# Queries of the dilated attention patterns copied residue by residue on GpSimd, for a stationary block without gaps

## The chip, the cores and the metric

One core of a Trainium2 chip runs the whole program in one launch. The metric is the device time of one execution in microseconds (us). Engines are named as in the profile: PE is TensorE's matmul part, PEld its weight load (the load of the stationary block), DVE VectorE, ACT ScalarE, POOL GpSimd, SP SyncE, which issues nearly all DMAs.

## What is computed

One layer of a hybrid decoder for a prompt of 2048 tokens (width 1024) and a group of 32 sample tokens. The part that matters here is the attention of the prompt: 8 heads of 64 dims, three patterns of (window, dilation), outputs merged by their softmax denominators.

```python
DIL_PATTERNS = ((128, 1), (512, 4), (2048, 16))

def _dilated_branch_prompt(q, k, v, dilation, slopes):
    qs = q.reshape(b, L, dilation, h, dh)      # token = j * dilation + c
    ks = k.reshape(b, L, dilation, h, dh)
    ...
    scores = jnp.einsum('bnqchd,bnkchd->bnchqk', qb, kb).astype(jnp.float32) * (HEAD_DIM ** -0.5)
    bias = -slopes[:, None, None] * (dilation * diff).astype(jnp.float32)[None]
    scores = jnp.where(valid[None, :, None, None], scores + bias[None, None, None], NEG)
    m = jnp.max(scores, axis=-1, keepdims=True)
    p = jnp.exp(scores - m)
    l = jnp.sum(p, axis=-1, keepdims=True)
    out = jnp.einsum('bnchqk,bnkchd->bnqchd', (p / l).astype(v.dtype), vb)
```

With dilation r the tokens fall into r residue classes c; within a class, 128 queries attend to their own block of 128 keys and the block before it. Around the attention stand an input projection with a pooling mixer (before it), and the output projection, a norm and a convolutional feed-forward (behind it).

## The kernel before

The stages follow one another: projections (to about 443 us), prompt attention head by head (443 to 841 us), merge of the patterns and output projection (to 1065 us), feed-forward (to the end). Products are made of a high and a low part of the numbers.

In the attention, a head's queries and keys lie in SBUF as the tile `QK`, [128, 3, 2048]: plane 0 holds the queries (64 rows high part, 64 rows low part), planes 1 and 2 the keys' high and low part. Columns are tokens in their natural order. There are two such tiles, so the next head's is loaded (by SP) during the current head.

The work of the attention is cut into 192 items (head h, pattern p, pair pr): 8 heads, 3 patterns (dilation 1, 4, 16; called p0, p1, p2 below), 8 pairs of query blocks. `advance(i)` issues three things:

- `scores` of item i: per block (idx = 2 * pr + s) two products into `Sp` in PSUM, L262 with the keys' high part and L263 with the low part. The stationary operand of both is the block of 128 queries, the moving operand the 128 or 256 keys. `views` cuts both out of `QK` with a stride of r columns: 1 in p0, 4 in p1 (16 bytes), 16 in p2 (64 bytes). Then DVE adds the bias table and finds the extreme (L265, tile `T`), ACT takes the exponential (L267, tile `Pt`).
- `turn` of item i - 2: PE transposes the blocks of `Pt` (L275), DVE or ACT copies them to SBUF (L278, L280, tile `PTs`).
- `values` of item i - 3: products with the values `V` (L296; fp32, so each is two instructions), copied out by ACT (L300), the extremes `st` by POOL (L302). Every fourth item a half of the pattern's output goes to HBM.

Per head p0 has 31 blocks of 128 keys by 128 queries, p1 28 and p2 16. So 128 blocks of p2 in all (8 heads x 16) and 32 of p1 (the 4 first of each head) have 128 keys, the other 96 of p1 have 256.

The order in which each engine's instructions stand is set at build time by the framework's scheduler; each engine then works its list off in order. POOL's list in this stage is short: 128x8 copies of `st`, memsets of a column in `V`, one bias table per head (L166). SP's list has the loads of `QK` and `V`, the stores of the outputs, small parameter rows (tile `row`), eight pieces of W_out for later (tile `rawo`), and a load of the pooling mixer's result (`act<-pl_s`).

Of the kernel before, what the change touches and what calls it, by code (L numbers as in the profile page):

```python
# [9 lines left out]
F32 = mybir.dt.float32  # L10
# [33 lines left out]
def kernel(ctx, tc, ins, cst, outs):  # L44
# [24 lines left out]
    nc.vector.memset(mhalf, -0.5)  # L69
    # the sample group's columns of a product stand side by side, hi then lo: one pass takes both  # L70
    mix_s = const.tile([P, 4, 2 * NSMP], F32R, name="mix_s")
# [22 lines left out]
    def norm_rows(pool, xt, g_bc, bufs, tag="xn"):  # L94
        """x * rsqrt(mean(x^2) + eps), times g_bc where given."""
        rows = xt.shape[0]
        xn = pool.tile([rows, DM], F32, tag=tag, name="xn", bufs=bufs)
        ss = pool.tile([rows, 1], F32, tag="ss", name="ss", bufs=2)
        nc.scalar.activation(xn, xt, AF.Square, accum_out=ss)
        r = rms_scale(pool, ss, 1, DM)  # L100
        if g_bc is None:
            nc.scalar.activation(xn, xt, AF.Copy, scale=r)
        else:
            nc.vector.scalar_tensor_tensor(out=xn, in0=xt, scalar=r, in1=g_bc[:rows], op0=ALU.mult, op1=ALU.mult)  # L104
        return xn
# [5 lines left out]
    def transpose_split(src, hi, lo):  # L111
        """src [n, DM] -> hi, lo [128, KT, n]."""
        n = src.shape[0]
        for h in range(2):
            tp = psum.tile([P, 4, P], F32, tag="tp", name="tp", bufs=4)
            for k in range(4):
                kk = 4 * h + k
                nc.tensor.transpose(tp[:, k, :n], src[:, kk * P:(kk + 1) * P], ident[:n, :n])  # L118
            split(hi[:, 4 * h:4 * h + 4, :], lo[:, 4 * h:4 * h + 4, :], tp[:, :, :n])
# [8 lines left out]
    class Later:  # L128
        """Work on the tensor engine that is issued some bursts of products after what it waits for."""

# [38 lines left out]
    def value_tile(pool, tag):  # L169
        """Pairs of heads, with a column of ones on either side (the sums of the weights)."""  # L170
        t = pool.tile([P, 16, P + 2], F32, tag=tag, name="V", bufs=3 if tag == "V" else 1)
        nc.gpsimd.memset(t[:, :, 0:1], 1.0)
        nc.gpsimd.memset(t[:, :, P + 1:P + 2], 1.0)
        return t
# [15 lines left out]
    def param_load(j):  # L190
        n = 2 * NF if j < 4 else 2 * SB
        row = rows_of[j] = p2.tile([2 * NF, 4 * P], F32, tag="row", name="row", bufs=3)
        if j < 4:
            src = conv_b if j == 3 else conv_w[0, j:j + 1]
            nc.sync.dma_start(row[:, 0:P], src.rearrange("l (c p) -> (l c) p", p=P))
        else:
            nc.sync.dma_start(row[:n], stv[:, (j - 4) * 4 * P:(j - 3) * 4 * P])
# [16 lines left out]
    def store_o(p, hp, O, half):  # L214
# [9 lines left out]
        else:  # L224
            eng.dma_start(dst.rearrange("(i c) f -> i c f", c=16)[:, s], O[:, s])

    def load_head(h):
        qk, tab = qk_tile(), bias_table(h)
        load_qk(h, qk, slice(0, S))
        heads[h] = (*(qk[:, i, :] for i in range(3)), tab)  # L230

    pair_v, pair_o, heads = {}, {}, {}

    def next_v(hp, p):
        pair_v[hp, p] = value_tile(p2, "V")
        load_v(hp, p, pair_v[hp, p])

    def views(h, p, idx):
        r = DILS[p]
        blk, c = divmod(idx, r)  # L240
        q, kh, kl = (x.rearrange("p (j c) -> p c j", c=r)[:, c, :] for x in heads[h][:3])
        lo = blk - 1 if blk else 0
        return (q[:, blk * P:(blk + 1) * P], kh[:, lo * P:(blk + 1) * P], kl[:, lo * P:(blk + 1) * P],
                ([idx - r] if blk else []) + [idx])
# [3 lines left out]
    def scores(it):  # L248
        h, p, pr = it
        tab = heads[h][3]  # L250
        if pr % 4 == 0:
            state["st"] = pq.tile([P, 8], F32, tag="st", name="st", bufs=4)
        st = state["st"]
        Sp = psum.tile([P, 2, 2 * P], F32, tag="mm", name="Sp", bufs=4)
        Pt = pq.tile([P, 2, 2 * P], F32, tag="P", name="Pt", bufs=4)
        blocks = []
        for s in range(2):
            idx = 2 * pr + s
            i8 = idx % 8
            q, kh, kl, kb = views(h, p, idx)  # L260
            w = P * len(kb)
            nc.tensor.matmul(Sp[:, s, :w], q, kh, start=True, stop=False)  # L262
            nc.tensor.matmul(Sp[:, s, :w], q, kl, start=False, stop=True)  # L263
            T = pq.tile([P, 2 * P], F32, tag="T", name="T", bufs=4)
            nc.vector.tensor_tensor_reduce(out=T[:, :w], in0=Sp[:, s, :w], in1=tab[:, p, 2 * P - w:], op0=ALU.add,  # L265
                                           op1=ALU.min, scale=1.0, scalar=3e38, accum_out=st[:, i8:i8 + 1])
            nc.scalar.activation(Pt[:, s, :w], T[:, :w], AF.Exp, bias=st[:, i8:i8 + 1], scale=-1.0)  # L267
            blocks += [(s, idx % 4, n, b, len(kb)) for n, b in enumerate(kb)]
        return st, Pt, blocks
# [38 lines left out]
    attn, PTs = {}, {}  # L308

    def advance(i):  # L310
        if i < len(items):
            attn[i] = scores(items[i])
        if 0 <= i - 2 < len(items):
            PTs[i - 2] = turn(items[i - 2], attn[i - 2])
        if 0 <= i - 3 < len(items):
            values(items[i - 3], attn.pop(i - 3), PTs.pop(i - 3))

# [1 line left out]
    right = ExitStack()  # L319
    pw = right.enter_context(tc.tile_pool(name="pw", bufs=1, side="right"))  # L320
    with tc.tile_pool(name="p1", bufs=1) as p1:
# [24 lines left out]
        def load_w(i):  # L346
            """Raw weights; the high part of the next ones takes their place."""
            j = JS[i]
            for c in range(KT // 2):
                raw[j, c] = (pw.tile([P, 2, AW], F32, tag=f"w{i}{c}", name="raw", bufs=1) if i < 3 else  # L350
                             p1.tile([P, 2, AW], F32, tag="x" if c == 2 else "ue", name="raw", bufs=2))
                nc.sync.dma_start(raw[j, c], wv[:, 2 * c:2 * c + 2, j * AW:(j + 1) * AW])

        def split_w(i):
            """hi + lo of gain * w."""
            j = JS[i]
# [120 lines left out]
        def window_sums(cur, g, pick, tag, shape, n):  # L477
            """Trailing sums over 2 << g columns by doubling; pick(tile, a, b) are the columns a..b-1."""
            sh = 1
# [148 lines left out]
    cw = const2.tile([P, 4, 2 * NF], F32, name="cw")  # L628
    # rows 0..15: the sample group's states (new ones take the place of the old), 16, 17: the prompt's
    stT = const2.tile([P, 2 * NF, 2 * SB + 2], F32, name="stT")  # L630
# [3 lines left out]
    def h_tile(k):  # L634
        """High and low part of 128 rows: of W_out at first, then of the normed tokens of a chunk."""
        return ph.tile([P, 2, TM], F32R, tag=f"h{k}", name="h", bufs=1)
# [12 lines left out]

# [1 line left out]
    with tc.tile_pool(name="p2", bufs=1, reuse_waits="tile") as p2:  # L651
        wo0 = [h_tile(k) for k in range(KT)]
        next_v(0, 1)
        next_v(0, 2)
        nc.vector.memset(stT[:, :, 2 * SB:], 0.0)
        for i in range(AHEAD, len(items) + 3):
            if i < len(items):
# [12 lines left out]
                if h == 6 and (8 * p + pr) % 3 == 0:  # L670
                    for k in ((8 * p + pr) // 3,):
                        raw = p2.tile([P, CH], F32, tag="row", name="rawo", bufs=3)
                        nc.sync.dma_start(raw, wov[:, k, 0:CH])
# [7 lines left out]
    with tc.tile_pool(name="p4", bufs=1, reuse_waits="tile") as p4:  # L681
# [19 lines left out]

# [1 line left out]
        wo = [[[wo0[k][:, b, 0:CH] for b in range(2)] for k in range(KT)], {}]  # L703
# [119 lines left out]

# [1 line left out]
        ST = p4.tile([P, 3, H, SB, SN], F32, name="ST")  # L825
# [19 lines left out]
        def cache_rows(c, b, n, p, near):  # L845
            """The 128 cached rows that query n of sequence b reads in pattern p, as [128, AW]."""
            if p == 0:
# [138 lines left out]
        def sample_mix():  # L986
            """Output projection, residual and norm of the sample group, then its columns hs_s."""
            y = smp["y"] = p4.tile([NSMP, DM], F32, tag="ya", name="ya", bufs=5)
# [48 lines left out]
        def store_ffn_state(j):  # L1037
            """New states of 512 columns, the sample group's and the prompt's."""
            tp = psum.tile([P, 4, P], F32, tag="tp", name="tpf", bufs=4)
# [17 lines left out]
        for c in range(NCHUNK):  # L1057
# [5 lines left out]
            def spread(pss, prompt, sample):  # L1063
                """Pairs (destination, PSUM source) of the prompt's and sample's columns."""
                if not last:
# [159 lines left out]
```

## Time and profile before

| what | value |
|---|---|
| median of 3 runs | 2590.65 us (2588.75 to 2595.58) |
| profiled execution, first to last instruction (span) | 2587.3 us |
| PE / PEld / DVE / ACT / POOL busy share of the span | 99% / 85% / 67% / 42% / 5% |
| prompt attention, from the first to the last score product | 443 to 841 us |
| DMA, mean over the span | 152 GB/s |

The profile gives of its own execution the span alone; the median of the runs stands 3.35 us above it. Busy time of PE counts overlapping matmuls by modelled ends, so a busy PE is not PE at its peak; how far apart instructions start says more. [...]

### The profile page before, as it was taken

The page shows a single profiled execution, that of the slowest core. Times are in us where ns is not written, and L with a number is a line of the kernel's source. Part 1 is how long each engine was busy: PE and PEld are TensorE (multiplying, and loading weights), DVE is VectorE, ACT ScalarE, POOL GpSimd, SP SyncE. Part 2 cuts the span into 40 slices and gives each one's busy share as a digit, 9 for nine tenths or more (in the row PEclk, how much of TensorE's full clock was granted, in tenths as well). Part 3 has the DMA queues.
Part 4 walks back from the last instruction along what each step waited for, and adds up shares of the span by engine and source line. Part 5 has one row for each costly group of instructions (what it writes and reads, how often), then busy time and mean ns, then how long its engine had stood idle before and what let it go on. Part 6 is the DMA issues. An engine that isn't in the chain of part 4 may idle for free.

```text
span 2587.3 us, 35898 instructions
## 1 busy us (share of the span) xinstructions
PE 2556.2 (99%) x13310; PEld 2187.1 (85%) x13310; DVE 1727.8 (67%) x3819; ACT 1089.6 (42%) x2021; POOL 117.4 (5%) x160
## 2 busy tenths in 40 slices
PE   8999999999999999999999999999999999999999
PEld 5888887999999788788888888888888788999997
DVE  7444345555555676799887788887887666666665
ACT  6333232555555222434433464443444443444442
POOL 1111111000000200000000000000000000000000
PEclk9999999998998999999999999999999999999999
DMA  6333335765561897955557534447443337232321
GB/s 220 106 118 112 121 110 149 153 174 131 125 160 51 294 309 244 298 183 183 181 165 233 157 106 146 137 128 246 143 138 114 122 110 232 84 90 83 91 75 61
DMA packets 411738, 393.57 MB, mean 152 GB/s; under 512 B 15211, under 2 KB 318407, under 8 KB 408876
## 3 DMA queue, kind: packets, MB, share of 16 engines
q1 hardware_dynamic: 411340, 390.48, 49.8%
q8 instruction: 105, 1.72, 0.3%
q0 software_dynamic: 224, 0.80, 0.1%
q14 instruction: 69, 0.57, 0.1%
HBM read 305.70 MB, written 85.52 MB: 151 GB/s over the span
## 4 chain that ended last, share of the span: by engine, by line
PE 62%; DMA 1%; DVE 1%; issue 0%; ACT 0%; SPq 0%; POOL 0%; POOLq 0%
PE pu L973 38%; PE pd L1149 19%; PE po L752 3%; PE pd L1143 1%; DMA om<-o_s 0%; DMA h<-hn_s 0%; PE sacc L925 0%; PE sacc L924 0%; PE po L1006 0%; DMA raw<-in_w_up_dram 0%; PE tp L118 0%; DMA h_s<-ya 0%; PE tpf L1041 0%; DVE xn L104 0%; PE tpa L737 0%
## 5 line engine op out<-in xcount | busy, mean ns | idle before, releaser
L973 PE MATMUL pu<-h,w 128*128 128x512 f32 (+1 forms) x5232 | 989.0, 349 | 1.5 <-ACT w L108 1.0
L973 PEld LDWEIGHTS pu<-h,w 128*128 128x128 f32 x5232 | 849.9, 188 | 132.4 <-ACT w L108 1.4
L1149 PE MATMUL pd<-w,act 128*128 128x512 f32 x2112 | 490.2, 392 | 0.0
L1149 PEld LDWEIGHTS pd<-w,act 128*128 128x128 f32 x2112 | 396.6, 188 | 88.1
L108 ACT CAST w<-raw 128x1024 fp32r<-128x1024 f32 (+1 forms) x282 | 286.9, 1026 | 293.0 <-PE pd L1149 189.7
L109 DVE TENSOR_TENSOR w<-raw,w 128x1024 fp32r<-128x1024 f32 (+1 forms) x278 | 328.6, 1185 | 23.9 <-ACT w L108 23.7
L422 PE MATMUL ps<-W_hi,xh 128*128 128x512 f32 x1024 | 332.1, 397 | 1.3 <-ACT xh L108 1.3
L1117 DVE SCALAR_TENSOR_TENSOR cv<-ex,cw,cv 128x512 f32<-128x512 f32 x352 | 262.3, 745 | 29.7 <-ACT cv L1109 27.2
L1107 ACT COPY ex<-pu 128x512 f32<-128x512 f32 (+1 forms) x220 | 110.1, 501 | 350.7 <-PE pu L973 350.3
L265 DVE CUSTOM_DVE_ANT_0 T<-Sp,tab 128x256 f32<-128x256 f32 (+1 forms) x384 | 132.0, 365 | 186.1 <-PE Sp L263 142.2
L422 PEld LDWEIGHTS ps<-W_hi,xh 128*128 128x128 f32 x1024 | 192.2, 189 | 43.4 <-ACT xh L108 2.0
L267 ACT ACTIVATE Pt<-T,st 128x256 f32<-128x256 f32 (+1 forms) x384 | 164.9, 458 | 136.4 <-DVE st L265 134.9
L422 PE MATMUL ps<-W_lo,xh 128*128 128x512 f32 x512 | 202.6, 396 | 0.0
L1151 DVE TENSOR_TENSOR ya<-ya,pd 128x512 f32<-128x512 f32 x192 | 131.0, 683 | 103.7 <-PE pd L1149 102.9
L296 PE MATMUL Op<-V,PTs 128*128 128x65 f32 x1200 | 174.8, 281 | 0.7 <-DVE PTs L278 0.6
L262 PE MATMUL Sp<-QK 128*128 128x256 f32 (+1 forms) x384 | 170.0, 453 | 5.5 <-DMA QK<-kT_hi 3.1
L296 PEld LDWEIGHTS Op<-V,PTs 128*128 128x128 f32 x1200 | 170.0, 209 | 1.2 <-DVE PTs L278 0.7
L1109 ACT ACTIVATE cv<-pu,cw 128x512 f32<-128x512 f32 (+3 forms) x264 | 166.0, 649 | 0.0
L91 POOL TENSOR_TENSOR rs<-ms,mhalf 128x1 f32<-128x1 f32 (+3 forms) x68 | 76.4, 1124 | 1582.7 <-DVE stT L1110 1046.9
L263 PE MATMUL Sp<-QK 128*128 128x256 f32 (+1 forms) x384 | 145.4, 387 | 0.6 <-DMA QK<-kT_lo 0.6
L275 PE MATMUL tp<-ident,Pt 128*128 128x128 f32 x600 | 127.7, 299 | 0.0
L108 ACT CAST act<-cv 128x512 fp32r<-128x512 f32 x88 | 54.6, 621 | 159.4 <-DVE cv L1126 150.7
(220 smaller groups left out, 2637.6 us busy)
## 6 DMA issues: line engine op xcount, KB each, us to landing
raw<-in_w_up_dram SPq DMA_DIRECT2D x176, 512.0 KB
raw<-in_w_down_dram SPq DMA_DIRECT2D x80, 512.0 KB
hn_s<-w SPq DMA_DIRECT2D x16, 1024.0 KB
h<-hn_s SPq DMA_DIRECT2D x32, 512.0 KB
far<-in_cache_k_dram SPq DMA_DIRECT2D x64, 256.0 KB
far<-in_cache_v_dram SPq DMA_DIRECT2D x64, 256.0 KB
om<-o_s SPq DMA_DIRECT2D x16, 792.0 KB
raw<-in_w_in_dram SPq DMA_DIRECT2D x16, 512.0 KB
```

The costliest lines, as they stand in the source:

```text
L108: nc.scalar.copy(hi, src)
L109: (eng or nc.vector).tensor_tensor(out=lo, in0=src, in1=f32(hi), op=ALU.subtract)
L262: nc.tensor.matmul(Sp[:, s, :w], q, kh, start=True, stop=False)
L263: nc.tensor.matmul(Sp[:, s, :w], q, kl, start=False, stop=True)
L265: nc.vector.tensor_tensor_reduce(out=T[:, :w], in0=Sp[:, s, :w], in1=tab[:, p, 2 * P - w:], op0=ALU.add, op1=ALU.min, scale=1.0, scalar=3e ...
L267: nc.scalar.activation(Pt[:, s, :w], T[:, :w], AF.Exp, bias=st[:, i8:i8 + 1], scale=-1.0)
L296: nc.tensor.matmul(Op[:, i4, :], PT[:, j, :], pair_v[hp, p][:, b, v0:v0 + DH + 1], start=n == 0, stop=n == m - 1)
L422: nc.tensor.matmul(ps, xh[:, a, k, :], (W_hi, W_lo)[b][j, k // 2][:, k % 2, :], start=n == 0, stop=n == 3 * KT - 1)
L973: nc.tensor.matmul(ps[:, :n], w[:, a, k, :], hs[k][:, b, c0:c0 + n], start=i == 0, stop=i == 3 * KT - 1)
L1109: nc.scalar.activation(d, s, AF.Identity, bias=cw[:, 3, ct:ct + 1], scale=cw[:, 2, ct:ct + 1])
L1117: nc.vector.scalar_tensor_tensor(out=d, in0=e[j], scalar=cw[:, j, ct:ct + 1], in1=d, op0=ALU.mult, op1=ALU.add)
L1149: nc.tensor.matmul(ps, act[0][:, a, k, tau * P:(tau + 1) * P], wd[k][:, b, :], start=k == 0 and j == 0, stop=k == n - 1 and j == 2)
```

## The change

GpSimd copies the queries of p1 and p2 into a new tile `qs`, half a pattern (1024 columns, 8 blocks) at a time, so that a block's 128 queries lie side by side. There are two such tiles and 32 copies (8 heads x 2 patterns x 2 halves). A copy is issued three items ahead of the first that reads it. The score products of p1 and p2 take their stationary block from `qs`; the moving keys still come from `QK` with the stride. To make room, `Pt` and `T` have 3 buffers in place of 4, `row` (also used by `rawo`) 2 in place of 3.

```diff
-        row = rows_of[j] = p2.tile([2 * NF, 4 * P], F32, tag="row", name="row", bufs=3)
+        row = rows_of[j] = p2.tile([2 * NF, 4 * P], F32, tag="row", name="row", bufs=2)
...
+    def spread_q(h, p, half):
+        qs = spread[h, p, half] = p2.tile([P, S // 2], F32R, tag="qs", name="qs", bufs=2)
+        q, r = heads[h][0], DILS[p]
+        if p == 1:
+            src = q[:, half * (S // 2):(half + 1) * (S // 2)].rearrange("p (b j c) -> p b c j", b=2, c=r)
+            dst = qs.rearrange("p (b c j) -> p b c j", b=2, c=r)
+        else:
+            src = q.rearrange("p (j c) -> p c j", c=r)[:, half * r // 2:(half + 1) * r // 2]
+            dst = qs.rearrange("p (c j) -> p c j", j=P)
+        nc.gpsimd.tensor_copy(dst, src)
...
+    def queries(h, p, idx):
+        if p == 0:
+            return heads[h][0][:, idx * P:(idx + 1) * P]
+        return spread[h, p, idx // 8][:, idx % 8 * P:(idx % 8 + 1) * P]
+
     def views(h, p, idx):
         r = DILS[p]
         blk, c = divmod(idx, r)
-        q, kh, kl = (x.rearrange("p (j c) -> p c j", c=r)[:, c, :] for x in heads[h][:3])
+        kh, kl = (x.rearrange("p (j c) -> p c j", c=r)[:, c, :] for x in heads[h][1:3])
         lo = blk - 1 if blk else 0
-        return (q[:, blk * P:(blk + 1) * P], kh[:, lo * P:(blk + 1) * P], kl[:, lo * P:(blk + 1) * P],
+        return (queries(h, p, idx), kh[:, lo * P:(blk + 1) * P], kl[:, lo * P:(blk + 1) * P],
                 ([idx - r] if blk else []) + [idx])
...
-        Pt = pq.tile([P, 2, 2 * P], F32, tag="P", name="Pt", bufs=4)
+        Pt = pq.tile([P, 2, 2 * P], F32, tag="P", name="Pt", bufs=3)
...
-            T = pq.tile([P, 2 * P], F32, tag="T", name="T", bufs=4)
+            T = pq.tile([P, 2 * P], F32, tag="T", name="T", bufs=3)
...
+    SPREAD = 3
+
     def advance(i):
+        if i + SPREAD < len(items):
+            h, p, pr = items[i + SPREAD]
+            if p and pr % 4 == 0 and i + SPREAD >= 2 * AHEAD:
+                spread_q(h, p, pr // 4)
         if i < len(items):
             attn[i] = scores(items[i])
...
+        for half in range(2):
+            spread_q(0, 1, half)
         for i in range(AHEAD, len(items) + 3):
```

On POOL, in the first head: the difference of the two lists, behind the first small copy of `st`. The memsets prepare value tiles `V`, `O_first<-st` and `O<-st` are small copies.

```order
 L172 MEMSET V 128x16
 L173 MEMSET V 128x16
+L237 COPY qs<-QK 128x1024
 L172 MEMSET V 128x16
 L173 MEMSET V 128x16
-L302 COPY O_first<-st 128x8
-L302 COPY O<-st 128x8 x4
+L237 COPY qs<-QK 128x1024
+L319 COPY O_first<-st 128x8
+L237 COPY qs<-QK 128x1024
+L319 COPY O<-st 128x8
```

Two query copies now stand ahead of the second small copy of `st`; from there on a query copy and a small copy alternate for a while, four query copies per head.

On PE, in p2 of the second head, the list of before (`Sp` score products, `tp` transposes, `Op` products with the values):

```order
L262 MATMUL Sp<-QK 128x128
L263 MATMUL Sp<-QK 128x128
L275 MATMUL tp_5034<-ident,Pt 128x128 x2
L296 MATMUL Op<-V,PTs 128x65 x2
L262 MATMUL Sp<-QK 128x128
L263 MATMUL Sp<-QK 128x128
L262 MATMUL Sp<-QK 128x128
L263 MATMUL Sp<-QK 128x128
```

and of the change:

```order
L279 MATMUL Sp<-QK,qs 128x128
L280 MATMUL Sp<-QK,qs 128x128
L292 MATMUL tp_5050<-ident,Pt 128x128 x2
L313 MATMUL Op<-V,PTs 128x65 x2
L279 MATMUL Sp<-QK,qs 128x128
L280 MATMUL Sp<-QK,qs 128x128
L279 MATMUL Sp<-QK,qs 128x128
L280 MATMUL Sp<-QK,qs 128x128
```

The rows stand in the same order; what differs is that the products also read `qs`, so that PE now waits for POOL's copy.

## Rows read from the trace of the kernel before

**Rows 1.** First part of the page: engine, busy us, share of the span, instructions.
```profile
PE 2556.2 (99%) x13310; PEld 2187.1 (85%) x13310; DVE 1727.8 (67%) x3819; ACT 1089.6 (42%) x2021; POOL 117.4 (5%) x160
```
**Rows 2.** Busy time by stretch: length, each engine's busy us (instructions), clock, DMA, GB/s.
```profile
443.00:841.00 398.00, 394.26 (x2585) 381.70 (x2586) 211.73 (x932) 213.28 (x533) 23.94 (x75) 0.89 0.57 137
```
**Rows 3.** PEld in order of time, p0 of the second head: start, us, line, operation.
```profile
500.29 0.19 PEld L262 LDWEIGHTS Sp<-QK 128*128 128x128 f32 x1 [0.34 <-DVE st L265]
500.40 0.19 PEld L263 LDWEIGHTS Sp<-QK 128*128 128x128 f32 x1
500.52 0.53 PEld L296 LDWEIGHTS Op<-V,PTs 128*128 128x128 f32 x4
```
**Rows 4.** PEld in order of time, p2 of the second head.
```profile
535.20 0.29 PEld L262 LDWEIGHTS Sp<-QK 128*128 128x128 f32 x1
535.39 0.31 PEld L263 LDWEIGHTS Sp<-QK 128*128 128x128 f32 x1
535.61 0.32 PEld L262 LDWEIGHTS Sp<-QK 128*128 128x128 f32 x1
535.84 0.31 PEld L263 LDWEIGHTS Sp<-QK 128*128 128x128 f32 x1
536.09 0.21 PEld L275 LDWEIGHTS tp<-ident,Pt 128*128 128x128 f32 x2
536.27 0.52 PEld L296 LDWEIGHTS Op<-V,PTs 128*128 128x128 f32 x4
536.85 0.30 PEld L262 LDWEIGHTS Sp<-QK 128*128 128x128 f32 x1
```
**Rows 5.** PE in order of time, p1 of the second head.
```profile
516.98 0.58 PE L262 MATMUL Sp<-QK 128*128 128x256 f32 x1
517.38 0.42 PE L263 MATMUL Sp<-QK 128*128 128x256 f32 x1
517.61 0.42 PE L262 MATMUL Sp<-QK 128*128 128x256 f32 x1
517.86 0.41 PE L263 MATMUL Sp<-QK 128*128 128x256 f32 x1
518.09 0.62 PE L275 MATMUL tp<-ident,Pt 128*128 128x128 f32 x4
```
**Rows 6.** PE in order of time, p2 of the second head.
```profile
535.20 0.46 PE L262 MATMUL Sp<-QK 128*128 128x128 f32 x1
535.49 0.39 PE L263 MATMUL Sp<-QK 128*128 128x128 f32 x1
```
**Rows 7.** Who waited for whom, 440 to 845 us: total us, times, longest.
```profile
PEld Sp L262 <- DVE st L265: 7.1, 20, 0.7
```
**Rows 8.** Groups of POOL by shape: busy us, mean ns of one.
```profile
L166 POOL TENSOR_SCALAR tab<-base 128x768 f32<-128x768 f32 x8 | 17.3, 2170 | 1.2 <-DMA base<-const_dram 1.0
L302 POOL COPY O<-st 128x8 f32<-128x8 f32 x44 | 9.0, 205 | 303.3 <-DVE st L265 294.8 <-DMA V<-v_s 8.5
```
**Rows 9.** POOL in order of time, first head.
```profile
453.32 0.19 POOL L302 COPY O_first<-st 128x8 f32<-128x8 f32 x1 [16.15 <-DVE st L265]
```
**Rows 10.** Groups of DVE while POOL made a bias table, 594.2 to 596.2 us, and before, 588 to 594.1 us.
```profile
L265 DVE CUSTOM_DVE_ANT_0 T<-Sp,tab 128x128 f32<-128x128 f32 x1 | 0.3, 292 | 0.2 <-PE Sp L263 0.2
L265 DVE CUSTOM_DVE_ANT_0 T<-Sp,tab 128x128 f32<-128x128 f32 x7 | 2.0, 292 | 3.5 <-PE Sp L263 2.7 <-PE tp L275 0.5
```
**Rows 11.** DVE and POOL in order of time, merge stage.
```profile
854.55 0.69 DVE L731 TENSOR_TENSOR at<-at,t 128x512 f32<-128x512 f32 x1
860.68 2.71 DVE L731 TENSOR_TENSOR at<-at,t 128x512 f32<-128x512 f32 x1
860.38 2.46 POOL L109 TENSOR_TENSOR w<-raw,w 128x1024 fp32r<-128x1024 f32 x1 [1.02 <-ACT w L108]
```
**Rows 12.** Busy time by stretch, second head: p2, its end, and the start of p0.
```profile
526.00:538.00 12.00, 11.94 (x80) 11.41 (x78) 6.65 (x32) 6.01 (x16) 0.57 (x4) 1.00 0.35 95
539.00:545.00 6.00, 6.00 (x31) 6.00 (x30) 2.74 (x15) 3.25 (x9) 0.71 (x2) 0.50 0.63 178
545.00:549.00 4.00, 4.00 (x21) 4.00 (x20) 1.46 (x7) 1.35 (x4) 1.62 (x1) 0.50 1.01 211
549.00:556.00 7.00, 7.00 (x62) 6.78 (x61) 4.81 (x20) 4.59 (x11) 0.37 (x3) 1.00 0.82 195
```

More of the change, by code (lines that the diff above doesn't have):

```diff
@@ L230, in load_head @@
         heads[h] = (*(qk[:, i, :] for i in range(3)), tab)
-    pair_v, pair_o, heads = {}, {}, {}
+    pair_v, pair_o, heads, spread = {}, {}, {}, {}
     def next_v(hp, p):
@@ L671 @@
                     for k in ((8 * p + pr) // 3,):
-                        raw = p2.tile([P, CH], F32, tag="row", name="rawo", bufs=3)
+                        raw = p2.tile([P, CH], F32, tag="row", name="rawo", bufs=2)
                         nc.sync.dma_start(raw, wov[:, k, 0:CH])
```

## The prediction

> **What bounds the kernel now.** I read the page first, then busy time by stretch, then single instructions of PE and its weight loads in order of time, then POOL. The page shows PE busy 99% of the span and POOL 5% [rows 1]. The change touches the prompt attention alone, 443 to 841 us: in these 398 us PE is busy 394.3 and PEld 381.7 us, DVE and ACT 212 and 213 us, POOL 23.9 us [rows 2]. So TensorE sets this stage, and its longest wait for another engine before a score product sums to only 7.1 us [rows 7]. The stages behind it are run by PE as well, and nothing in them is tied to a date: a microsecond saved here should move them forward whole.
>
> Within TensorE, look at how far apart weight loads start, since they run one after another while matmuls overlap them. In p0, where queries lie side by side, loads start 0.11 and 0.12 us apart and last 0.19 us [rows 3]. In p2, where they lie 64 bytes apart, the four loads of an item start 0.19 to 0.25 us apart (0.89 us for four steps, 0.22 each) and last 0.29 to 0.32 us [rows 4]. Same instruction, same 128 columns; only the stride differs. That is what the change removes. [...]
>
> **The change part by part.**
>
> Score products with 128 keys. There are 160 strided blocks of this kind (128 in p2, 32 in p1) with two loads each, 320 loads. A step falls from 0.22 us to what is then the longer of the load (0.11 to 0.12) and the matmul over 128 strided key columns. The latter is not shown alone. From below it is bounded by the contiguous step, 0.11. From above by half of what 256 strided columns take at most, 0.23 to 0.25 us a step in p1 [rows 5], so 0.12. I take 0.12: 320 x 0.10 = **32 us**. If instead such a matmul took the whole 0.22, as a rival assumes, this would shrink.
>
> Score products with 256 keys, 96 blocks in p1. Steps inside a chain of four are 0.23 to 0.25 us, and the last one, whose next load is a contiguous one for a transpose, is still 0.23 [rows 5]; so the moving keys, still strided, seem to hold it, and contiguous queries win nothing there. But the first product of a chain stands 0.40 us ahead of the second in p1 and 0.29 us in p2, where there are half the keys [rows 5, 6]: one load that nothing hides (0.2), plus the matmul. That load loses 0.10. In PE's list 75 of the 96 blocks start such a chain: 75 x 0.10 = **7.5 us**. Between nothing for the rest and a drop to the contiguous step (0.11 less, on 192 products less those 75) lie 0 and 13 us; I take 0, nearest to the 0.23 of that last step.
>
> Query copies, 32 on POOL. No row shows a strided copy. The nearest is the bias table, 128x768 in 2.17 us, 2.8 ns a column, so 2.9 us for 1024 [rows 8]. From above: TensorE pays twice for a stride [rows 3, 4], which would make 5.8 us; far above, the 128x8 copies take 205 ns, 26 ns a column [rows 8], nearly all fixed cost. I take 3 us, 96 us in all beside 398 us in which POOL works 24: hidden. When must a copy be ready? There are two tiles, so the copy for a half starts when the half before the last has been read, four items ahead of its first reader. An item of p2 takes 1.65 us now (first load to first load, 535.20 to 536.85) [rows 4] and about 1.65 - 4 x 0.10 = 1.25 us after. Four of these are 5 us, against 3. In p1 there is more. At the start, POOL's first small copy ends at 453.5 us [rows 9]; two copies behind it end at about 459.5, and p1 begins at about 460 and needs the second half four items later. In POOL's list a small copy that waits for DVE stands between query copies, but these waits are for items that PE has passed by then. So **0 us**.
>
> [...] POOL's copies might slow DVE. In the merge stage a DVE operation with two operands in SBUF took 2.71 us in place of 0.69 while POOL worked [rows 11]. But the score operation L265 has one operand in PSUM, and beside POOL's bias table it took 292 ns, as it did before [rows 10]. The eight splits of W_out pieces in the seventh head have two SBUF operands; POOL will be busy some three eighths of that time, so 3 of them lose 2 us, most of it in DVE's slack: **+2 us**.
>
> Fewer buffers. `Pt` of item i+3 can be overwritten when the transposes of item i are issued, which stand ahead of it in PE's list anyway. `T` with three buffers lets DVE run three blocks ahead of ACT; both are half idle. `row` is needed once in eight items. I count these at 0, and hide the risk in the next term. SP's list changes in that `act<-pl_s` (2 MB) stands some rows earlier, ahead of the third head's `QK` load, whose reader is a head away: 0.
>
> New stalls. DVE's and ACT's 212 us will have to fit in some 358 us, so PE will come early more often; the 7.1 us of waits grow, I say, by **+5 us** (nothing to 15).
>
> The clock. In the second head the granted clock falls from 1.0 to 0.5 near the end of p2, after a stretch with 80 PE instructions in 12 us, and comes back 4 us into p0; at 0.5 the rate is 31 in 6 us and 21 in 4, against 62 in 7 us behind [rows 12]. The stage's mean of 0.89 [rows 2] means 22% of it, 88 us, at the low level. With shorter loads p2 has more matmul work per microsecond and is a quarter shorter, so the falls should come less often. If they went altogether, an item would win some 0.4 us (the level raises transposes and value products, not the strided loads) on the 35 to 40 items in such stretches, 15 us; if they stay, 0. I take about half, **-8 us**.
>
> Sum: -32 - 7.5 + 2 + 5 - 8 = -40.5 us. The span would be 2546.8; with the 3.35 us by which the median stands above it, 2550.2, so **2550 us**.
>
> **Rivals.**
>
> (a) The moving keys bind: a matmul over 128 columns 64 bytes apart takes as long as the load, 0.22. Then only chain starts win: 113 of the 160 narrow blocks and 75 wide ones, 188 x 0.10 = 19 us, less the 5 of stalls and 2 of contention: about 2579 us. For it: the keys stay strided. Against it: a chain starts 0.29 us ahead of its second product with 128 keys, 0.40 with 256 [rows 5, 6], so 128 more columns cost about 0.11.
>
> (b) The moving keys cost nothing, and what I read as their price in p1 was the loads': another 13 us in p1, and full clock, 7 us: about 2530 us. Against it is the step of 0.23 ahead of a contiguous load. [...]
>
> (c) The stride does not matter and the long loads come from something else in p1 and p2: no gain, contention and stalls cover each other, 2591 us. The rows at equal columns [rows 3, 4] speak against it. [...]
>
> (d) POOL is too slow, and slower is the result: PE waits for `qs` at the second half of p2 once a copy takes over 5 us, at its first half over some 7.2 us (four items of p1). Loss per head (C - 5) + (C - 7.2); at C = 8.5 us it eats 38 us, all of the gain. Beyond that the kernel is slower: at 11 us by 78 - 40, some 2629 us. For it: no strided POOL read is in the trace. Against it: C would have to be three times the bias table's price per column.
>
> (e) DVE and ACT catch up with PE in p2, so that half of the narrow term is lost: about 2566 us.
>
> **How the numbers follow.** Forecast 0.60, (a) 0.10, (b) 0.10, (c) 0.05, (d) 0.07, (e) 0.08. The range reaches from (b), with 4 us below it, to just short of (a): 2526 to 2577; it leaves out most of (a), (c), (d). A change of 0.3%, 7.8 us, is about what a measurement of this kernel can tell from none. Faster are the forecast, (a), (b), (e): 0.88, less a little for the edges, 0.87; same (c) 0.05 and that edge, 0.06; slower (d) 0.07.
>
> **What would show it.** Weight loads of the score products at 186 to 192 ns in all patterns; steps of about 0.12 us in p2 and still 0.23 in the middle of p1; query copies of 2.5 to 4 us; no wait of a score product for `qs` worth more than 2 us in all; the attention done in about 358 us with a mean clock of 0.92 or more. I am wrong if p2's steps stay near 0.22, if the copies last over 5 us, or if the time shows up again in the merge stage.

## The result and the profile after

| what | before | after |
|---|---|---|
| median of 4 runs each, side by side | 2589.73 us (2588.75 to 2595.58) | 2545.68 us (2542.25 to 2547.30) |
| ratio, 95% interval | | 0.9825 [0.9811, 0.9839] |
| span of the profiled execution | 2587.3 us | 2545.4 us |
| first to last score product | 443.1 to 841.2 us (398.1) | 441.8 to 796.3 us (354.5) |

The change saves 44 us between the medians and 45 by the ratio, 1.75%; the forecast was 2550 us. In the two profiled executions the span fell by 41.9 us: the attention took 43.6 us less and started 1.3 us earlier, and the stages behind it took 3.0 us more (1746.1 us from the last score product to the end before, 1749.1 after).

The page of after, busy time by engine (compare [rows 1]):

```profile
PE 2509.0 (99%) x13310; PEld 2133.0 (84%) x13310; DVE 1728.4 (68%) x3819; ACT 1086.4 (43%) x2021; POOL 180.5 (7%) x192
```

Busy time by stretch of after, the attention and what lies behind it (compare [rows 2]):

```profile
core 0: us, PE busy (x) PEld busy (x) DVE busy (x) ACT busy (x) POOL busy (x), PEclk, DMA share, GB/s
441.00:797.00 356.00, 346.80 (x2592) 327.57 (x2592) 210.46 (x933) 210.07 (x533) 86.71 (x107) 0.93 0.64 154
797.00:2546.00 1749.00, 1733.81 (x8667) 1459.13 (x8665) 1303.56 (x2406) 711.36 (x1179) 21.48 (x23) 1.00 0.51 161
```

POOL has 63 us more work, PEld 54 us less, and TensorE still sets the stage. DVE and ACT do what they did before.

Weight loads of after in p2 of the second head, in order of time (compare [rows 4]):

```profile
523.98 0.19 PEld L279 LDWEIGHTS Sp<-QK,qs 128*128 128x128 f32 x1
524.09 0.19 PEld L280 LDWEIGHTS Sp<-QK,qs 128*128 128x128 f32 x1
524.20 0.19 PEld L279 LDWEIGHTS Sp<-QK,qs 128*128 128x128 f32 x1
524.31 0.19 PEld L280 LDWEIGHTS Sp<-QK,qs 128*128 128x128 f32 x1
524.45 0.21 PEld L292 LDWEIGHTS tp<-ident,Pt 128*128 128x128 f32 x2
524.63 0.52 PEld L313 LDWEIGHTS Op<-V,PTs 128*128 128x128 f32 x4
525.21 0.19 PEld L279 LDWEIGHTS Sp<-QK,qs 128*128 128x128 f32 x1
```

A load lasts 0.19 us in place of 0.29 to 0.32, the steps are 0.11 us in place of 0.22, and an item takes 1.23 us (523.98 to 525.21) in place of 1.65. The matmuls over 128 strided keys, which the steps of p2 also hold, fit in 0.11 us.

Matmuls of after in p1 of the second head (compare [rows 5]):

```profile
508.17 0.46 PE L279 MATMUL Sp<-QK,qs 128*128 128x256 f32 x1
508.45 0.41 PE L280 MATMUL Sp<-QK,qs 128*128 128x256 f32 x1
508.68 0.41 PE L279 MATMUL Sp<-QK,qs 128*128 128x256 f32 x1
508.91 0.41 PE L280 MATMUL Sp<-QK,qs 128*128 128x256 f32 x1
```

Only the first step of the chain is shorter, 0.28 us in place of 0.40; the others stay at 0.23.

The groups of POOL in the attention of after, by line (busy us, mean ns | idle time before them and what ended it):

```profile
L237 POOL CAST qs<-QK 128x1024 fp32r<-128x1024 f32 x32 | 64.5, 2014 | 143.7 <-PE Sp L280 110.2 <-issue 18.1 <-PE Sp L279 15.4
```

A copy takes 2.01 us. It is the copies that wait for PE, for a free `qs`; a wait of PE for `qs` does not show.

Waits of after in the attention (engine, line, waited for: us in total, times, longest us; compare [rows 7]):

```profile
PEld Sp L279 <- DVE st L282: 8.6, 24, 0.7
...
ACT h L108 <- DMA rawo<-in_w_out_dram: 4.4, 4, 2.7
DVE h L109 <- ACT h L108: 4.1, 4, 2.3
```

The wait for DVE hardly grew. The wait for `rawo` was 0.5 us before: pieces of W_out, which share the smaller `row`, now come late in the seventh head. Where that meets PE, in order of time:

```profile
707.80 0.62 ACT L108 CAST h<-rawo 128x512 fp32r<-128x512 f32 x1 [2.66 <-DMA rawo<-in_w_out_dram]
708.33 0.90 ACT L284 ACTIVATE Pt<-T,st 128x256 f32<-128x256 f32 x2
...
708.88 0.44 PE L292 MATMUL tp<-ident,Pt 128*128 128x128 f32 x2 [2.28 <-ACT Pt L284]
```

ACT, working its list off in order, waits 2.66 us for the piece, the exponentials stand behind it, and PE waits 2.28 us for them.

### The profile page after: what moved, and what is told of

Read it like the earlier page. It is cut to its first block, busy times and chain, and to the rows that moved or that the text cites. A ratio compares the mean times of both kernels' runs of the same rounds, so it can differ in the third digit from the quotient of the medians.

```text
span 2545.4 us, 35989 instructions
## 1 busy us (share of the span) xinstructions
PE 2509.0 (99%) x13310; PEld 2133.0 (84%) x13310; DVE 1728.4 (68%) x3819; ACT 1086.4 (43%) x2021; POOL 180.5 (7%) x192
## 4 chain that ended last, share of the span: by engine, by line
PE 93%; DMA 2%; DVE 2%; issue 1%; ACT 1%; POOL 0%; SPq 0%; DVEq 0%; POOLq 0%; ACTq 0%
PE pu L998 38%; PE pd L1174 19%; PE ps L445 13%; PE po L777 5%; PE Op L313 5%; PE Sp L279 3%; PE tp L292 3%; PE Sp L280 2%; PE tp L118 1%; PE tp L454 1%; PE pd L1168 1%; DVE W_lo L388 1%; DMA QK<-kT_lo 0%; PE pp L519 0%; DMA ya<-in_x_prompt_dram 0%
## 5 line engine op out<-in xcount | busy, mean ns | idle before, releaser
L313 PEld LDWEIGHTS Op<-V,PTs 128*128 128x128 f32 x1200 | 163.6, 202 | 2.7 <-DVE PTs L295 2.0
L445 PEld LDWEIGHTS ps<-W_lo,xh 128*128 128x128 f32 x512 | 96.8, 189 | 20.0
L1135 DVE COPY stT<-ex 128x2 f32<-128x2 f32 x176 | 28.8, 164 | 114.8 <-ACT ex L1132 114.8
```

Of the source, the lines that this page charges most:

```text
L313: nc.tensor.matmul(Op[:, i4, :], PT[:, j, :], pair_v[hp, p][:, b, v0:v0 + DH + 1], start=n == 0, stop=n == m - 1)
L445: nc.tensor.matmul(ps, xh[:, a, k, :], (W_hi, W_lo)[b][j, k // 2][:, k % 2, :], start=n == 0, stop=n == 3 * KT - 1)
```

## The experiments

Each run is compared with the kernel before on the same chip; ratios are to that kernel.

**1. Buffers alone.** The kernel before with the smaller `Pt`, `T` and `row`, and no copies.

```diff
-        ... tag="row", name="row", bufs=3)
+        ... tag="row", name="row", bufs=2)
-        ... tag="P", name="Pt", bufs=4)
+        ... tag="P", name="Pt", bufs=3)
-            ... tag="T", name="T", bufs=4)
+            ... tag="T", name="T", bufs=3)
```

> The kernel before with the smaller buffers alone (Pt and T 3, row 2), no copies, queries still strided. Theory (the gain is the shorter weight loads): 2588 to 2596 us, no gain; score weight loads stay at 290 to 337 ns in p1 and p2. Rival (the gain comes from the other order that the smaller buffers give): some 2550 to 2575 us.

Measured: 2588.75 us, ratio 1.0003 [0.9993, 1.0014]. The buffers cost nothing at the pace of the kernel before.

**2. Copies that nobody reads.** The change, but the products of p1 and p2 take their queries from `QK` as before.

```diff
     def queries(h, p, idx):
-        if p == 0:
-            return heads[h][0][:, idx * P:(idx + 1) * P]
+        if p >= 0:
+            r = DILS[p]
+            blk, c = divmod(idx, r)
+            return heads[h][0].rearrange("p (j c) -> p c j", c=r)[:, c, blk * P:(blk + 1) * P]
```

> The change, but the products of p1 and p2 take their queries from QK with the stride again; the 32 copies are made and read by nobody. Theory (copies are hidden): 2588 to 2598 us, POOL 64 us more. Rival (the copies slow DVE or hold POOL's list, and the change wins in spite of them): over 2600 us. Rival (something else than the reading of the copy wins): below 2580 us.

Measured: 2590.52 us, ratio 1.0007 [0.9996, 1.0019]. POOL is busy 86.6 us in the attention, as in the changed kernel, and it costs at most what the interval leaves, about 5 us. This kernel differs from the changed one only in where the products read their queries, so everything that was won comes from reading the copies.

**3 and 4. One pattern alone.** `queries` as in experiment 2 for the pattern that is left out, and its copies gone.

```diff
-        if p == 0:
+        if p != 2:
...
-            if p and pr % 4 == 0 and i + SPREAD >= 2 * AHEAD:
+            if p == 2 and pr % 4 == 0 and i + SPREAD >= 2 * AHEAD:
```

> The change for p2 alone: p1 takes strided queries and has no copies. Theory (0.10 us per weight load, and the clock falls less often): 256 loads, 25.6 us, and most of the clock's share, 5 to 10 us: 2552 to 2562 us; weight loads 186 to 192 ns in p2, about 310 to 337 in p1. Rival (the clock brings most, and p2 sets the clock): 2545 to 2550 us, all of the gain.

> The change for p1 alone: p2 takes strided queries and has no copies. Theory (64 loads of narrow blocks and 75 chain starts at 0.10 us): 14 us, 2573 to 2580 us, and the clock still falls in p2 of each head. Rival (the clock brings most): within 4 us of the kernel before.

Measured: p2 alone 2559.98 us, 0.9889 [0.9872, 0.9905]; p1 alone 2575.95 us, 0.9950 [0.9933, 0.9966]. On the 2587.67 us of the kernel before beside them that is 28.7 us [24.6, 33.1] and 12.9 us [8.8, 17.3], together 41.6 of the 45: the two add up. Both are in the ranges of their theories. By the steps read above it would be 256 loads of p2 x 0.11 = 28 us, and 64 loads x 0.11 and 75 chain starts x 0.12 = 16 us in p1. The measured figures also hold what the clock gave, and the two are not separated: the granted clock of a whole run is 0.982 in the mean before, 0.984 with p1 alone, 0.988 with p2 alone and 0.989 with both. Where p2 begins and p1 ends in the second head, the kernel with p2 alone has both kinds of load beside each other, copied queries (`qs`) and strided ones:

```profile
524.78 0.19 PEld L281 LDWEIGHTS Sp<-QK,qs 128*128 128x128 f32 x1
524.89 0.19 PEld L282 LDWEIGHTS Sp<-QK,qs 128*128 128x128 f32 x1
525.04 0.31 PEld L281 LDWEIGHTS Sp<-QK 128*128 128x128 f32 x1
525.26 0.33 PEld L282 LDWEIGHTS Sp<-QK 128*128 128x128 f32 x1
```

**5. Keys without a stride too.** What do the moving keys cost, which stayed strided?

```diff
-        kh, kl = (x.rearrange("p (j c) -> p c j", c=r)[:, c, :] for x in heads[h][1:3])
+        kh, kl = heads[h][1:3]
```

> The change, and p1 and p2 also read their moving keys without a stride: 128 or 256 neighbouring columns of QK, which are the wrong keys (the dilation of the keys is left out). Theory (with the stationary block packed, the strided moving keys hold the 192 wide products of p1 at 0.235 us, and nothing in p2): wide steps fall to some 0.115 us, 192 x 0.12 = 23 us less than the change, 2518 to 2528 us; p2 steps stay at 0.11 to 0.12. Rival (the wide step has another cause): 2543 to 2548 us.

Measured: 2524.48 us, 0.9750 [0.9736, 0.9765], 21 us under the changed kernel by the medians. Matmuls in p1 of the second head:

```profile
506.67 0.36 PE L279 MATMUL Sp<-QK,qs 128*128 128x256 f32 x1
506.87 0.28 PE L280 MATMUL Sp<-QK,qs 128*128 128x256 f32 x1
506.99 0.28 PE L279 MATMUL Sp<-QK,qs 128*128 128x256 f32 x1
507.11 0.28 PE L280 MATMUL Sp<-QK,qs 128*128 128x256 f32 x1
507.22 0.49 PE L292 MATMUL tp<-ident,Pt 128*128 128x128 f32 x3
```

The steps fall from 0.23 to 0.12 us, the first from 0.28 to 0.20. So 256 strided keys cost 0.23 us, 256 adjacent ones 0.12. Over p1 that is 117 inner steps x 0.11 and 75 first ones x 0.08, 19 us, of the 21 measured.

**6. A copy four times as long.** Each copy is made four times over, to see what PE loses when it does have to wait for POOL.

```diff
-        nc.gpsimd.tensor_copy(dst, src)
+        for _ in range(4):
+            nc.gpsimd.tensor_copy(dst, src)
```

> The change with each query copy made four times in a row, 8.1 us in place of 2.0. Prediction's rival (d): PE then waits (8.1 - 5) + (8.1 - 7.2) = 4 us per head, 32 us, so 2570 to 2585 us. Other theory (the real slack of a copy is larger than four items, or only the second half of p2 is tight): 2544 to 2560 us. If a copy held up POOL's whole list: over 2590 us.

Measured: 2605.96 us, 1.0067 [1.0052, 1.0082], 60 us over the changed kernel (16 over the kernel before beside it), above the ranges of both theories. The third case, that a copy holds up POOL's whole list, names this range, but its mechanism does not show: among the waits of PE for POOL there are only those for `qs`. Waits in the attention; the two rows from PE and its loads are mostly the same stalls, seen from two queues:

```profile
POOL qs L238 <- PE Sp L281: 58.5, 22, 6.7
...
PEld Sp L280 <- POOL qs L238: 29.9, 18, 5.4
...
PE Sp L280 <- POOL qs L238: 26.3, 16, 5.2
```

Busy time of the stretch:

```profile
443.00:858.00 415.00, 384.44 (x2601) 365.91 (x2601) 219.72 (x935) 215.03 (x535) 276.76 (x204) 0.82 0.55 132
```

For a half of 4 x 2.01 = 8.0 us the prediction's rival (d) gives (8.0 - 5) + (8.0 - 7.2) = 3.8 us a head, 30 us in all, and the waits are 29.9. That the totals agree is luck. Read one by one in the list of weight loads, the waits are 2.0 to 3.0 us in each of the second to sixth heads, less than the formula says; 7.3 us fall in the first head, 5.4 of them ahead of its first block of p1, and 7.9 in the last, where p2 comes ahead of p1.

The waits are also not the whole loss. The mean clock is 0.82 in place of 0.93. With levels of 1.00 and 0.50, as in [rows 12], that is 36% of 415 us, about 149 us, at 0.5 against 14% of 356, about 50. PE is busy 384.4 us in this stretch and 346.8 in that of the changed kernel, for the same products. So of the 59 us by which the stretch is longer, some 38 are slower instructions, which fits the lower clock, and some 21 are idle time.

**7. The `row` buffer back.** `row` and `rawo` have 3 buffers again, and `PTs` 3 in place of 4 makes the room.

```diff
-        ... tag="row", name="row", bufs=2)
+        ... tag="row", name="row", bufs=3)
-        PT = pq.tile([P, 4, P], F32, tag="PTs", name="PTs", bufs=4)
+        PT = pq.tile([P, 4, P], F32, tag="PTs", name="PTs", bufs=3)
```

> The change with row back at 3 buffers and PTs at 3 in place of 4 (room for it). Theory (the wait of PE for an exponential behind a W_out piece in the seventh head, 2.3 us, and the slow clock behind it come from row at 2): the wait is gone, 2 to 5 us less than the change, 2540 to 2544 us. Rival (the order of the loads on SP makes it, or PTs at 3 costs as much): 2544 to 2549 us.

Measured: 2542.19 us, 0.9821 [0.9804, 0.9837]. The wait for `rawo` falls from 4.4 to 2.1 us, the medians differ by 3.5 us, but the intervals overlap: a gain of that size is not resolved. The wait of PE for the exponential is not gone, as the theory had it: it is 1.4 us in place of 2.3. So the smaller `row` makes at most a part of it. The mean clock from 443 to 860 us is 0.95, against 0.93 in the changed kernel.

**8. The keys of p1 copied as well.** For heads 1 to 7 POOL copies the strided keys of p1, high and low part, in four pieces during p2 of the head before, into 16 KB a partition that the pooling mixer's result takes later. The load of the pooling mixer's result moves from p2 to p0 of the last head.

```diff
+    def spread_k(h, part):
+        if part == 0:
+            t = ph.tile([P, 2, 4, CH], F32R, tag="act", name="ks", bufs=1)
+            keys[h] = t
+        i, half = divmod(part, 2)
+        js = slice(half * CH // 2, (half + 1) * CH // 2)
+        nc.gpsimd.tensor_copy(keys[h][:, i, :, js], heads[h][1 + i].rearrange("p (j c) -> p c j", c=4)[:, :, js])
...
+        if p == 1 and h in keys:
+            kh, kl = (keys[h][:, i, c, :] for i in range(2))
...
+                if h < 7 and p == 2 and pr % 2 == 1:
+                    spread_k(h + 1, pr // 2)
-                if (h, p, pr) == (7, 2, 0):
+                if (h, p, pr) == (7, 0, 0):
```

> The change, and in heads 1 to 7 GpSimd also packs the keys of p1 (4 copies of 1024 columns per head, made during p2 of the head before) into the 16 KB that the pooling mixer's result takes later; its load moves to the last head's p0. Theory (as for the unstrided keys, seven heads of eight): 84 blocks x 2 x 0.12 = 20 us less than the change, 2521 to 2532 us. Rival (POOL's longer list makes PE wait for qs, or the late load holds up the merge): 2540 us or more.

Measured: 2527.50 us (2523.26 to 2532.28), 0.9764 [0.9748, 0.9780], 18 us under the changed kernel by the medians, and the fastest version that computes everything. Seven eighths of the 19 us of experiment 5 are 17. Matmuls in p1 of the second head:

```profile
510.35 0.36 PE L289 MATMUL Sp<-ks,qs 128*128 128x256 f32 x1
510.55 0.28 PE L290 MATMUL Sp<-ks,qs 128*128 128x256 f32 x1
510.67 0.38 PE L302 MATMUL tp<-ident,Pt 128*128 128x128 f32 x2
```

and the key copies on POOL, 2.10 us each, for which nobody waits:

```profile
L245 POOL CAST ks<-QK 128x1024 fp32r<-128x1024 f32 x28 | 57.9, 2100 | 30.0 <-PE Sp L290 25.0 <-issue 5.0
```

**9. From which stride on is it dear?** p1 takes its keys two columns apart in even heads and three in odd ones, with copied queries; p2 takes its queries two or three apart from `QK`.

```diff
     def queries(h, p, idx):
+        if p == 2:
+            n = 2 + h % 2
+            return heads[h][0][:, 0:n * P].rearrange("p (j c) -> p c j", c=n)[:, 0, :]
...
+        if p == 1:
+            n = 2 + h % 2
+            kh, kl = (x[:, 0:n * 4 * P].rearrange("p (j c) -> p c j", c=n)[:, 0, :] for x in heads[h][1:3])
...
-            if p and pr % 4 == 0 and i + SPREAD >= 2 * AHEAD:
+            if p == 1 and pr % 4 == 0 and i + SPREAD >= 2 * AHEAD:
```

> A measurement, with wrong queries and keys (other columns of QK). p1: packed queries, moving keys with a step of 2 columns (8 bytes) in even heads, 3 (12 bytes) in odd ones. p2: queries straight from QK with a step of 2 in even heads, 3 in odd ones, no copies. Theory A (any step over one column halves the rate, to 0.21 to 0.24 us): score weight loads near 300 ns in p2 of all heads, wide steps of p1 near 0.235 us in all heads. Theory B (the price grows with the distance up to 16 bytes): between the packed and the strided values, 3 dearer than 2; at 2 within 20 ns of packed.

One run, 2549.67 us. Weight loads of p2 in the first head (queries two apart) and in the second (three apart):

```profile
482.14 0.19 PEld L285 LDWEIGHTS Sp<-QK 128*128 128x128 f32 x1
482.25 0.20 PEld L286 LDWEIGHTS Sp<-QK 128*128 128x128 f32 x1
482.37 0.20 PEld L285 LDWEIGHTS Sp<-QK 128*128 128x128 f32 x1
482.49 0.20 PEld L286 LDWEIGHTS Sp<-QK 128*128 128x128 f32 x1
...
525.11 0.25 PEld L285 LDWEIGHTS Sp<-QK 128*128 128x128 f32 x1
525.28 0.26 PEld L286 LDWEIGHTS Sp<-QK 128*128 128x128 f32 x1
525.45 0.26 PEld L285 LDWEIGHTS Sp<-QK 128*128 128x128 f32 x1
525.62 0.26 PEld L286 LDWEIGHTS Sp<-QK 128*128 128x128 f32 x1
```

and matmuls of p1 in the third head (keys two apart):

```profile
551.51 0.46 PE L285 MATMUL Sp<-QK,qs 128*128 128x256 f32 x1
551.79 0.41 PE L286 MATMUL Sp<-QK,qs 128*128 128x256 f32 x1
552.02 0.42 PE L285 MATMUL Sp<-QK,qs 128*128 128x256 f32 x1
552.26 0.42 PE L286 MATMUL Sp<-QK,qs 128*128 128x256 f32 x1
```

The stationary load is free at a step of two (0.12 us apart), pays a part at three (0.17) and all at four and sixteen (0.19 to 0.25 in the kernel before). These loads read `QK` itself, so it is not the new tile that makes them short. The moving operand pays all of it at two already: 0.23 to 0.24 us, as at four; in the second head, at three, it is 0.23 as well. So the two theories each hold for one of the operands.

**10. Experiments 7 and 8 together.**

> The kernel with the keys of p1 copied too, and row and PTs at 3 buffers each as in the seventh run. Theory (the two gains stand side by side): 3 us less than with the keys alone, 2521 to 2527 us. Rival (the wait at the W_out pieces had gone already): 2526 to 2531 us. Either would be the fastest kernel here.

Measured: 2532.87 us (2528.49 to 2533.82), 0.9793 [0.9776, 0.9811]: no gain over experiment 8, and above the ranges of both theories. The longest wait of a score load for DVE's `st` is 3.5 us, against 0.9 in experiment 8, so one `PTs` less may cost what the third `row` gives; that was not taken apart.

## Why the prediction was right

The forecast was 2550 us and -40.5; the runs gave 2545.68 and -45, within the range. By its steps:

- **Narrow products and chain starts**, -39.5 predicted. The steps came out at 0.11 and 0.28 us, against 0.12 and 0.30 taken, which makes 320 x 0.11 + 75 x 0.12 = 44 us from steps rounded to 0.01. That is too much by some 6 us: 53 of the 320 products start in stretches at a clock of 0.5, where a copied block loads no faster than a strided one (0.21 to 0.24 us apart against 0.21 to 0.23, last section). With 267 in place of 320 it is 38 us, close to the forecast. Experiments 3 and 4 gave 41.6 together, the clock's share among them. No other part of the change gains anything: experiments 1 and 2, buffers and copies without their reader, stay within 0.2% of the kernel before. Rival (c), that the stride does not matter, is contradicted by the same load at 0.19 us packed and 0.29 to 0.32 us strided.
- **Wide products**, 0 predicted inside a chain: the step stayed at 0.23 us. That the moving keys hold it, which the prediction read from one last step, experiment 5 showed by taking their stride away. It also settles rivals (a) and (b): moving keys have a price, 0.11 us for 256, against (b); and with 128 of them, still strided, the steps of p2 are 0.11 us, against (a).
- **Query copies**, 3 us each and hidden. They took 2.01 us; the term was mis-sized and the sum did not hang on it. Rival (d) had the right sum of waits (30 us at 8 us a copy, 29.9 measured) by luck, since they are spread otherwise over the heads, and too low a total: it priced the waits alone, and in experiment 6 the lost time was twice that, with the clock at 0.82. Its point of no gain, 8.5 us a copy, is therefore too high: at 8.0 us the kernel is already 16 us slower than before.
- **Contention**, +2. The score operation of DVE takes 365 ns in the mean before and after; the eight splits of W_out went from 686 to 811 ns, 1 us in all. Experiment 2 bounds the rest. It cost more right behind the attention (last point).
- **Buffers**, 0. True at the old pace (experiment 1). In the faster kernel the pieces of W_out come late, which stops PE for 2.3 us once; with the third `row` back it is still 1.4 us (experiment 7), so the smaller buffer is not the whole cause, and the shares are open. This small term was missed; the +5 for stalls covered it, since the wait for DVE rose by only 1.5 us (7.1 to 8.6), and rival (e) did not come about.
- **The clock**, -8 for half of the low stretches. The mean of the attention went from 0.89 to 0.93, that is from about 88 to about 50 us at 0.5. The 0.4 us an item behind the prediction's price is seen in the trace of before: in the second head an item of p2 takes 2.08 us at 0.50 (first load to first load, 540.87 to 542.95) against 1.65, and of these the four steps of its strided loads take 0.95 us against 0.89. By that price, 15 us for 88, the 38 us are worth some 6 us. Among the 32 recorded runs of the kernel before in the experiments, the time grows by 0.24 us for each us more at 0.5, by which they are worth 9. Both are estimates, no run isolates it.
- **What lies behind** was to move forward whole. It gave 3.0 us of the 43.6 back. The trace shows most of it in the first 25 us of the merge, where PE waits for `at`, made by DVE, 4.80 us in place of 2.85, and another 0.65 us longer for ACT's `mh`. The lines of before and, behind the dots, of after:

```profile
859.95 0.69 DVE L726 TENSOR_TENSOR t<-om,E 128x512 f32<-128x512 f32 x1
863.54 1.09 PE L737 MATMUL tpa<-ident,at 128*128 128x128 f32 x4 [2.85 <-DVE at L731]
...
815.85 2.74 DVE L751 TENSOR_TENSOR t<-om,E 128x512 f32<-128x512 f32 x1
821.49 1.09 PE L762 MATMUL tpa<-ident,at 128*128 128x128 f32 x4 [4.80 <-DVE at L756]
```

  The same DVE operation with two operands in SBUF takes 2.74 us in place of 0.69. POOL works beside it without a gap in after (three splits of weights, 812.88 to 820.79); before, it started in a gap of POOL, ahead of the split of [rows 11]. In experiment 2, with the copies unread, the stages behind take as long as after the change, within 0.1 us; in experiment 1, without copies, 3.6 us less. So this goes with the copies and not with the shorter loads; how they move POOL's splits stays open. Time that shows up again in the merge stage was one of the prediction's signs of being wrong; it did, with 3 us.

## What to carry to other kernels

Where the same TensorE instruction takes longer in one place than in another, compare the operands' strides: a stationary block read with gaps doubled the distance between loads here (0.22 us against 0.11), and where loads set the pace an idle engine can pack it ahead of time. Pack the moving operand as well where it is long enough to bind, as here with 256 columns (0.23 us strided, 0.12 adjacent). Before relying on another engine's copies, work out when the buffer comes free and when its first reader stands in line, and expect that a wait can cost more than its own length, as in experiment 6 (29.9 us of waits, 60 us of time).

## What the runs showed of the hardware

- The two operands of a matmul bear a stride differently. For 128 fp32r columns, steps of the stationary load are 0.11 to 0.12 us at a column step of 1 and 2, 0.17 at 3, and 0.19 to 0.25 at 4 and 16. For 256 moving columns it is 0.12 us at 1 and 0.23 to 0.24 at 2, 3 and 4. The kernels before and after show theirs at a granted clock of 1.00; the runs of experiments 5 and 9 have 0.99 in the mean. So a step of two columns, 8 bytes, cost the stationary load nothing and the moving operand all of it. Why the two differ, no run shows.
- Packing the stationary block shortened the steps here at a clock of 1.00 (0.11 us against 0.22), not at 0.50. In p2 of the last head, where the granted clock is 0.50 from 748 to 771 us, copied blocks load 0.21 to 0.24 us apart; in the kernel before, also at 0.50, strided ones stand 0.21 to 0.23 apart (796.53 to 797.19 us). The lines of after:

```profile
753.45 0.33 PEld L279 LDWEIGHTS Sp<-QK,qs 128*128 128x128 f32 x1
753.67 0.33 PEld L280 LDWEIGHTS Sp<-QK,qs 128*128 128x128 f32 x1
753.88 0.33 PEld L279 LDWEIGHTS Sp<-QK,qs 128*128 128x128 f32 x1
```

- A strided copy of 1024 columns on POOL takes 1.92 to 2.09 us, 2.0 ns a column, at gaps of 16 bytes (p1) and of 64 (p2) alike within these bounds, less than the 2.8 ns of the bias table's operation [rows 8].
- Some 30 us of waits of PE for POOL went with 60 us of time and a mean clock of 0.82 against 0.93 (experiment 6); PE was busy 38 us longer with the same products. In the changed kernel the clock also falls behind the one stall of 2.3 us, with a mean of 0.57 from 709 to 716 us.
